# Attention gates and outputs stored by channel, reciprocals spread on GpSimd, and a filter network on 128 partitions

## The chip, the core and the metric

The kernel runs on one core of one Trainium2 chip. A core has TensorE (PE, with its weight load PEld), VectorE (DVE), ScalarE (ACT), GpSimd (POOL) and SyncE (SP). Each engine has a queue of its own that runs in order; engines wait for each other by semaphores. PE writes to PSUM only, and POOL reads and writes SBUF only. The metric is the device time of one execution in microseconds (us), the median of several runs.

## The reference, cut to what matters

One inference step of two layers on 1024 sample tokens and 128 prompt tokens, width 1024. Layer one is a Hyena long convolution, whose filters come from a small network; layer two is latent attention with 16 heads and a SiLU gate on each branch.

```python
def hyena_filters(L, w1, b1, freq, w2, b2, w3):      # L = 1024 and 128
    z = ...                                           # (L, 33) positions
    hdn = jnp.sin(fr * (z @ w1 + b1))                 # 33 -> 64
    hdn = jnp.sin(fr * (hdn @ w2 + b2))               # 64 -> 64
    h = hdn @ w3                                      # 64 -> 2048
    ...

def mla_latent(h, ckv_ctx, kpe_ctx, ...):
    q_a, kv_a, k_pe, gate = split(h @ w_in)           # 384, 256, 32, 1024
    q = rmsnorm(q_a) @ w_qb                           # 16 heads x (64 + 32)
    q_pe, k_pe = axial rope of the 32
    k_nope, v = expand(rmsnorm(kv_a)), with 256 cached tokens appended
    o = softmax(q k / sqrt(96)) @ v                   # 16 heads x 64
    return (o * silu(gate)) @ w_o
```

The prompt is attended to by itself alone, without rope. Residual, output gate and a last rmsnorm follow.

## The kernel before, in words

Nine tiles of 128 tokens (T = 1152; tile 8 is the prompt). Large products run as three matmuls on split operands: `hi` copies a value to the rounded type fp32r, `lo` subtracts that copy from the value, and hi x hi, hi x lo and lo x hi add up in one PSUM bank. So each operand costs an evacuation by two engines.

Start (`hyena`, L644 on): nine tiles of x are loaded, normalized and turned; eight 1 MB pieces of `ada_w` give scale and shift; `modulate` (L206) makes the parts hT and lT. Two input weights are applied early (L715): the first accumulates in three banks `ip_ps`, the second in three banks `sf_ps`, which the turned x and then the filter network use before it. `filters` (L235) runs the network with `sin_layer` (L211), feature on partition: 33 and 64 rows, tokens in pieces of 512, 512 and 128. A piece is a matmul, seven DVE instructions (L219 to L224, three of them L102) that scale and reduce the angle, and ACT's sine. Its result `hs` holds the high part in rows 0 to 63 and the low part in rows 64 to 127.

Attention (`mla`, L844): `w_out` ends the Hyena layer and normalizes its tiles one after the other into lhh and lhl (the hT and lT of this layer). `mla_gate` (L949) multiplies them with a quarter of the gate weights, for each token tile: tokens on PSUM's partitions, 256 channels in its columns. It stores silu of it to DRAM tiles `gate0` to `gate8`, one per token tile. The first quarter is emitted after `w_out`, the others after `mla_in`. `attend` (L959) copies the turned rope keys `kr` to four places of kT, six of the copies by DMA on SP. `attention` (L1049) runs four groups of four heads, each in four chunks of 256 queries (the last with 128 prompt queries as well), each chunk in four units of one head, order 0, 2, 1, 3. On PE, DVE and ACT the order inside is written out by hand (`ORDER`, `tc.manual_schedule`); POOL's and SP's queues, and all the rest, are ordered at build time by a planner that simulates the program. A unit does the scores and softmax of the next head, and transposes, products with V and the close of its own. Step `r` takes the reciprocal of the sums (L1177); `et` (L1182) adds V's high and low halves into `ot`, 64 channels by 256 queries, and POOL multiplies the gate by the reciprocals, one number per query, so queries stand on partitions there. After a second, odd unit, `fm` (L1211) turns the pair's `ot` to queries on partitions, `fx` (L1214) copies it from PSUM and POOL multiplies it with the gate. After four units `store_o` writes 256 queries by 256 channels to `og` tiles, one per token tile. The next chunk's `q_proj` (L1028) makes its rope from two copies, in which halves of 32 rows are swapped by DMA on SP, and POOL multiplies and splits; the first chunk's part stands ahead of all scores.

Output (`out_load`, `out_t`, `mla_out`): POOL splits the first half of `w_o` during the last chunk. `out_t` loads `og`, turns it by PE transposes (`split_t`, L835) to channels on partitions and splits it with ACT and DVE: first for tiles 0 to 3, then 8, 4, 5, then 6, 7. Then `mm3` (L616) projects.

Of the kernel before, what the change touches and what calls it, by code (L numbers as in the profile page):

```python
# [17 lines left out]
P = 128  # L18
# [57 lines left out]
class K:  # L76
# [134 lines left out]
    def sin_layer(self, pool, ps, w, src, kk, out, col):  # L211

        for o, n in ((0, 512), (512, 512), (1024, 128)):
            pt = ps.tile([P, 512], F32, name=STAG[0], tag=STAG[0], bufs=STAG[1])[0:64]
            self.PE.matmul(pt[:, :n], w, src[:kk, o:o + n], start=True, stop=True)
            x = pool.tile([64, 512], F32, name="mlp_x", tag="mlp_x")
            q = pool.tile([64, 512], F32, name="mlp_q", tag="mlp_q", bufs=1)
            x, q = x[:, :n], q[:, :n]
            self.V.tensor_scalar(x, pt[:, :n], self.fcol[:, col:col + 1], self.fcol[:, 0:1], ALU.add, ALU.mult)  # L219
# [15 lines left out]
    def filters(self, pool, ps, hs):  # L235

        nc, tc, a = self.nc, self.tc, self.a
        zt = pool.tile([33, T], F32, name="zt", tag="ft", bufs=2)
        nc.scalar.dma_start(zt, a["zemb"])
        w1 = pool.tile([33, 64], F32, name="w1", bufs=1)  # L240
        nc.scalar.dma_start(w1, a["f_w1"])
        w2 = pool.tile([64, 64], F32, name="w2", bufs=1)
        nc.scalar.dma_start(w2, a["f_w2"])
        fcol = pool.tile([64, 3], F32, name="fcol", bufs=1)
        nc.scalar.dma_start(fcol, a["f_cols"])
        self.fcol = fcol
# [597 lines left out]
    def mla(self, lh, hT, lT, wp, wo, gd, AB):  # L844
        tc, dr = self.tc, self.dr
        GD = [dr.tile([P, D], F32, name=f"gate{t}") for t in range(NT)]
        OG = [dr.tile([P, D], F32, name=f"og{t}") for t in range(NT)]
        with self.pool("mcs", space=PSUM) as ps:
# [99 lines left out]

    def mla_gate(self, h, pool, ps, hT, lT, GD, bufs):  # L949
        wh, wl = self.load_w(self.a["wm_g"][h], pool, 256, "wm", bufs, raw_bufs=2, step=1, tag_raw="wm_raw",  # L950
                             size=336 if h else 256)
        for t in range(NT):
            pt = ps.tile([P, 512], F32, name="wo_ps", tag="wo_ps", bufs=4)
            self.mm3(pt[:, :256], hT, lT, slice(P * t, P * t + P), wh, wl, 8)
            g = pool.tile([P, 256], F32, name="gsil", bufs=GB)
            self.S.activation(g, pt[:, :256], AF.Silu)
            (self.nc.sync if h else self.nc.scalar).dma_start(GD[t][:, 256 * h:256 * h + 256], g)
# [70 lines left out]
    def q_proj(self, m, c, part):  # L1028
# [8 lines left out]
        for i in range(2):  # L1037
            x = m["pool"].tile([P, 384], F32, name=f"rot{i}", bufs=1)[:, :n]
            self.S.copy(x, pt[:, :n])
            for r in range(0, P, 64):  # L1040
                y = r + 32 * i, r + 32 - 32 * i
                self.nc.sync.dma_start(x[y[1]:y[1] + 32], x[y[0]:y[0] + 32])
            self.tt(x, x, c["rq"][:, :n], ALU.mult, self.G)
            for r, j in ((slice(0, 64), i), (slice(64, P), i + 2)):
                self.hi("pool", qh[r, j, :n], x[r])
                self.lo("pool", ql[r, j, :n], x[r], qh[r, j, :n])
        yield

    def attention(self, m):  # L1049
# [3 lines left out]
        def start(n):  # L1053
# [6 lines left out]
            for i in range(2):  # L1060
                nc.sync.dma_start(gt[:, i], m["GD"][q0 // P + i][:, 256 * G:256 * G + 256])
# [3 lines left out]
            return c, [self.q_proj(m, c, p) for p in range(3)]  # L1065
# [90 lines left out]
    def step(self, m, u, what, n):  # L1156
# [19 lines left out]
        elif what == "r":  # L1176
            self.V.reciprocal(u["sm"][:, :, 3], u["sm"][:, :, 0])  # L1177
# [4 lines left out]
        elif what == "et":  # L1182
            self.halves(m["ot"], u["po"][:, :256], m["ov"], u["odd"])
            for i in range(2):
                o = gt[:, i, VH * j:VH * j + VH]
                self.G.tensor_scalar(o, o, u["sm"][:, i, 3:4], None, ALU.mult)  # L1186
            if u["odd"]:
                g = gt.rearrange("p i (e j d) -> p i e j d", e=2, d=VH)[:, :, :, j % 2]
                m["fin"] = [u["po"][:, 256:512], m["ot"], g, u if u["last"] else None]
        elif what in ("fm", "fx"):  # L1190
            self.finish(m, what)
# [12 lines left out]
    def finish(self, m, what):  # L1204
# [3 lines left out]
        pt, ot, g, u = m["fin"]  # L1208
# [11 lines left out]
    def store_o(self, m, c):  # L1220
        for i in range(2):
            self.nc.sync.dma_start(m["OG"][c["q0"] // P + i][:, 256 * c["G"]:256 * c["G"] + 256], c["gt"][:, i])

    def prompt(self, m, c):
# [4 lines left out]
        o = slice(256 * c["G"], 256 * c["G"] + 256)  # L1229
        g = pool.tile([P, 256], F32, name="gp", bufs=1)  # L1230
        self.nc.sync.dma_start(g, m["GD"][8][:, o])
# [20 lines left out]
        self.lo("dve", l, pt, h)  # L1252
        self.V.reciprocal(sm, sm)
        self.tt(heads(g), heads(g), sm.unsqueeze(2).broadcast_to([P, 4, VH]), ALU.mult, self.G)
# [9 lines left out]
        for odd in range(2):  # L1264
            self.half(ov, heads(po)[:, odd::2], odd)
        yield
        for odd in range(2):
            self.halves(ot, heads(po)[:, odd::2], ov, odd)
        yield
        for i in range(2):  # L1270
            self.PE.transpose(po[:, P * i:P * i + P], ot[:, i], self.ident)
        yield
        yield
        self.tt(g, po[:, :256], g, ALU.mult)
        self.nc.sync.dma_start(m["OG"][8][:, o], g)
# [32 lines left out]
    def out_t(self, ps, OG, pool, tiles, oh, ol):  # L1308
        for b in range(0, 8, 2):
            src = []  # L1310
            for t in tiles:
                x = pool.tile([P, 256], F32, name="og_in", bufs=4)
                self.nc.sync.dma_start(x, OG[t][:, P * b:P * b + 256])
                src.append(x)
            for k in range(2):
                self.split_t(ps, [x[:, P * k:P * k + P] for x in src], 0, oh, ol, b + k)

    def out_head(self, ps, OG, e):
        self.out_t(ps, OG, e["pool"], range(4), *e["o"])

    def mla_out(self, ps, OG, e, gd):
        nc, a = self.nc, self.a
        with self.pool("ew", 2, side="left") as pool:
# [5 lines left out]
            for tiles in (range(4), (8, 4, 5), (6, 7)):  # L1329
                if tiles[0]:  # L1330
                    oh, ol = (pool.tile([P, 8, 384], F32R, name=n) for n in ("oh", "ol"))
                    self.out_t(ps, OG, pool, tiles, oh, ol)
# [118 lines left out]
def _layout(i):  # L1451
# [16 lines left out]
    out["wm_a"], out["wm_g"] = _ktiles(wi[:, :672], 336), _ktiles(wi[:, 672:], 256)  # L1468
# [8 lines left out]
    out["w_o"] = _ktiles(i["mla_w_o"][0], 512)  # L1477
# [19 lines left out]
```

## Time and profile before

| | us |
|---|---|
| median of 3 runs (lowest, highest) | 1804.11 (1803.85, 1807.5) |
| profiled execution | 1801.83 |
| its span | 1799.7 |
| PE busy | 1747.2 (97%) |
| DVE busy | 1249.6 (69%) |
| ACT busy | 1088.1 (60%) |
| POOL busy | 528.1 (29%) |

The span runs from the first instruction to the last; the profiled execution's own time adds what lies around it. A row of the trace gives the start and the length in us, the engine, the line of the kernel, the operation, the tile written and the tiles read, and the shapes. Behind it stands, in brackets, how long the engine sat idle before and what released it. An engine name with a q is its queue issuing a DMA.

### The profile page before, as it was taken

The page shows a single profiled execution, that of the slowest core. Times are in us where ns is not written, and L with a number is a line of the kernel's source. Part 1 is how long each engine was busy: PE and PEld are TensorE (multiplying, and loading weights), DVE is VectorE, ACT ScalarE, POOL GpSimd, SP SyncE. Part 2 cuts the span into 40 slices and gives each one's busy share as a digit, 9 for nine tenths or more (in the row PEclk, how much of TensorE's full clock was granted, in tenths as well). Part 3 has the DMA queues.
Part 4 walks back from the last instruction along what each step waited for, and adds up shares of the span by engine and source line. Part 5 has one row for each costly group of instructions (what it writes and reads, how often), then busy time and mean ns, then how long its engine had stood idle before and what let it go on. Part 6 is the DMA issues. An engine that isn't in the chain of part 4 may idle for free.

```text
span 1799.7 us, 30649 instructions
## 1 busy us (share of the span) xinstructions
PE 1747.2 (97%) x11064; PEld 1568.3 (87%) x11064; DVE 1249.6 (69%) x2526; ACT 1088.1 (60%) x2582; POOL 528.1 (29%) x748
## 2 busy tenths in 40 slices
PE   6999999999999999999999899999999999999998
PEld 4888988999899888889999799999989999998786
DVE  3948797898886797432241587878787787878454
ACT  7655565755664234234452588878887887888332
POOL 2433333343344120331000233333423242344100
PEclk9999999999999999999999999999999999999999
DMA  8333332111122857322122300110101010002541
GB/s 325 94 113 106 115 107 74 51 54 45 61 101 92 293 188 260 135 82 91 55 67 80 90 27 24 35 29 20 35 25 29 20 37 17 28 27 68 187 135 71
DMA packets 94704, 157.15 MB, mean 87 GB/s; under 512 B 11671, under 2 KB 64183, under 8 KB 92760
## 3 DMA queue, kind: packets, MB, share of 16 engines
q1 hardware_dynamic: 91744, 151.78, 25.5%
q10 hardware_dynamic: 2552, 3.39, 0.6%
q8 instruction: 87, 1.43, 0.3%
q14 instruction: 65, 0.53, 0.1%
q0 software_dynamic: 256, 0.02, 0.0%
HBM read 113.89 MB, written 36.73 MB: 84 GB/s over the span
## 4 chain that ended last, share of the span: by engine, by line
PE 75%; DVE 11%; DMA 4%; ACT 4%; issue 3%; POOL 2%; SPq 0%; ACTq 0%; DVEq 0%; POOLq 0%
PE wo_ps L616 18%; PE wo_ps L1289 12%; PE ip_ps L415 11%; PE av_ps L1174 8%; PE nm_ps L1162 7%; PE wo_ps L989 5%; PE iv_ps L545 3%; PE df_ps L364 2%; DMA wi_raw<-w_in 2%; PE nm_ps L1021 1%; DVE pr_o L99 1%; DVE cv L102 1%; PE ada_ps L113 1%; POOL wi_l L96 1%; DVE mx L1292 1%
## 5 line engine op out<-in xcount | busy, mean ns | idle before, releaser
L1289 PE MATMUL wo_ps<-kT,qT 128*128 128x512 f32 (+1 forms) x1152 | 279.7, 373 | 8.1 <-ACT prob L1296 4.1
L1296 ACT ACTIVATE prob<-wo_ps,mx 128x512 f32<-128x512 f32 (+1 forms) x384 | 234.0, 618 | 17.9 <-DVE mx L1294 16.0
L88 ACT ACTIVATE pt_h<-nm_ps 128x512 fp32r<-128x512 f32 x324 | 192.9, 599 | 70.5 <-PE nm_ps L1162 63.2
L1292 DVE TENSOR_REDUCE mx<-wo_ps 128x1 f32<-128x512 f32 (+1 forms) x384 | 212.8, 594 | 27.9 <-PE wo_ps L1289 27.1
L1289 PEld LDWEIGHTS wo_ps<-kT,qT 128*128 128x128 f32 x1152 | 188.2, 190 | 42.6 <-ACT prob L1296 14.0
L96 DVE TENSOR_TENSOR pt_l<-nm_ps,pt_h 128x512 fp32r<-128x512 f32 x324 | 210.5, 682 | 13.2 <-ACT pt_h L88 13.1
L1162 PE MATMUL nm_ps<-ident,prob 128*128 128x128 f32 x1280 | 191.5, 272 | 0.0
L96 POOL TENSOR_TENSOR wi_l<-wi_raw,wi_h 128x512 fp32r<-128x512 f32 x64 | 110.7, 1730 | 253.0 <-ACT wi_h L88 237.0
L1162 PEld LDWEIGHTS nm_ps<-ident,prob 128*128 128x128 f32 x1280 | 150.1, 140 | 8.4
L415 PE MATMUL ip_ps<-lT,wi_h 128*128 128x384 f32 x720 | 152.3, 341 | 0.0
L415 PE MATMUL ip_ps<-hT,wi_h 128*128 128x384 f32 x720 | 150.8, 344 | 0.6 <-ACT cv L497 0.6
L415 PE MATMUL ip_ps<-hT,wi_l 128*128 128x384 f32 x720 | 150.7, 341 | 0.0
L1174 PE MATMUL av_ps<-pt_h,Vt 128*128 128x256 f32 x640 | 138.0, 297 | 0.0
L1174 PE MATMUL av_ps<-pt_l,Vt 128*128 128x256 f32 x640 | 135.4, 293 | 0.3 <-DVE pt_l L96 0.2
L415 PEld LDWEIGHTS ip_ps<-hT,wi_h 128*128 128x128 f32 x720 | 126.3, 190 | 6.9 <-issue 3.0
L415 PEld LDWEIGHTS ip_ps<-hT,wi_l 128*128 128x128 f32 x720 | 126.0, 188 | 7.1 <-issue 3.8
L415 PEld LDWEIGHTS ip_ps<-lT,wi_h 128*128 128x128 f32 x720 | 127.9, 190 | 3.7 <-issue 0.8
L616 PE MATMUL wo_ps<-wm_h,lhh 128*128 128x256 f32 (+1 forms) x432 | 125.9, 296 | 1.7 <-ACT wm_h L88 1.4
L616 PE MATMUL wo_ps<-wm_h,lhl 128*128 128x256 f32 (+1 forms) x432 | 127.1, 295 | 0.0
L616 PE MATMUL wo_ps<-wm_l,lhh 128*128 128x256 f32 (+1 forms) x432 | 126.7, 294 | 0.0
L1186 POOL TENSOR_SCALAR gt<-gt,sm 128x64 f32<-128x64 f32 x128 | 54.9, 443 | 225.3 <-DVE sm L1177 224.0
L99 POOL TENSOR_TENSOR pr<-ev 128x256 f32<-128x256 f32 x72 | 83.6, 1166 | 126.0 <-ACT ev L372 77.5
(338 smaller groups left out, 4060.1 us busy)
## 6 DMA issues: line engine op xcount, KB each, us to landing
wi_raw<-w_in SPq DMA_DIRECT2D x64, 256.0 KB, 2.6
ada_w<-ada_w SPq DMA_DIRECT2D x12, 1024.0 KB, 10.0
ada_w<-ada_w SPq DMA_DIRECT2D x24, 512.0 KB, 4.0
x_in<-xs SPq DMA_DIRECT2D x16, 512.0 KB, 5.3
PS<-pr_o SPq DMA_DIRECT2D x64, 128.0 KB, 1.9
pi_raw<-PS SPq DMA_DIRECT2D x32, 256.0 KB, 4.8
YD<-yv SPq DMA_DIRECT2D x8, 576.0 KB, 3.3
y<-YD SPq DMA_DIRECT2D x8, 576.0 KB, 8.7
```

Source lines behind the costliest of these rows:

```text
L88: self.S.activation(out, src, AF.Copy)
L96: e.tensor_tensor(out, src, hi.bitcast(F32), ALU.subtract)
L99: (eng or self.V).tensor_tensor(out, x, y, op)
L415: mm = self.PE.matmul(pt, w[:, k, :], x[c][:, k, :], start=s == 0 and k == 0, stop=s == 2 and k == 7)
L616: self.PE.matmul(pt, x[k][:, sl], w[:, k, :], start=s == 0 and k == 0, stop=s == 2 and k == kt - 1)
L989: self.PE.matmul(pt[:, :n], x[:, k, o:o + P], y[:, k, c], start=s == 0 and k == 0, stop=s == 2 and k == kt - 1)
L1162: self.PE.transpose(pt[:, P * i:P * i + P], u["p"][i % 2][n // 2][:, P * (2 * (n % 2) + i // 2):P * (2 * (n % 2) + i // 2) + P], self.ident)
L1174: self.PE.matmul(u["po"][:, :256], m["V"][:, 2 * n + e, j, :], u[n][1 + s][:, 256 * e:256 * e + 256], start=n == first and e + s == 0, sto ...
L1186: self.G.tensor_scalar(o, o, u["sm"][:, i, 3:4], None, ALU.mult)
L1289: self.PE.matmul(pt[:, :n], x[:, j, P * i:P * i + P], y[:, j, o:o + n], start=s == 0, stop=s == 2)
L1292: self.V.tensor_reduce(mx[:, b:b + 1], c["s", i, b][:, :n], AX.X, ALU.max)
L1296: self.S.activation(c["p"][i][b], c["s", i, b][:, :n], AF.Exp, bias=c["mx"][i][:, 3:4], accum_out=c["sm"][:, i, b:b + 1])
```

## The change

- The network takes two halves of 576 tokens at once, on rows 0 to 63 and 64 to 127: w1 as two blocks in zeroed tiles, w2 block diagonal, in two pieces of 288 columns a layer. POOL fills zt, w1 and w2 with zeros first, and the low half of `hs` is put together by five instructions where two were.
- The gate product is turned: weights stand still and tokens stream, 384 at a time, so that gate and output tiles in DRAM are one per 128 channels. Channels of w_in's gate and of w_o are reordered on the host to fit.
- The reciprocals are spread by POOL over 64 columns per head (`rr`), and PE transposes `rr` where it transposed `ot`. POOL multiplies the gate by it, then by `ot`, and issues the store, once per pair.
- `out_t` loads channels on partitions: no transposes. POOL splits the first four tiles, ACT and DVE the rest.
- The first chunk's rope swaps halves with DVE copies from PSUM; DVE multiplies, ACT and DVE split. kT's six DMAs go by POOL's queue.

```diff
-        for o, n in ((0, 512), (512, 512), (1024, 128)):
+        n = T // 4
+        for o in (0, n):
+            pt = ps.tile([P, 512], F32, name=STAG[0], tag=STAG[0], bufs=STAG[1])[:, :n]
+            for i, w in enumerate(ws):
+                self.PE.matmul(pt, w, src[:, 2 * n * i + o:2 * n * i + o + n], start=i == 0, stop=i == len(ws) - 1)
...
+        zt = pool.tile([P, T], F32, name="zt", bufs=1)
+        self.G.memset(zt, 0.0)
+        nc.scalar.dma_start(zt[0:33], a["zemb"])
...
+        for i in range(2):
+            r = slice(64 * i, 64 * i + 64)
+            nc.scalar.dma_start(w1[0:33, i, r], a["f_w1"])
+            nc.scalar.dma_start(w2[r, r], a["f_w2"])
+            nc.scalar.dma_start(fcol[r], a["f_cols"])
...
+        self.hi("act", hs[top, 0:n], h2[top])
+        self.hi("act", hs[low, n:T], h2[low])
+        self.S.copy(hs[top, n:T], hs[low, n:T].bitcast(F32))
+        self.lo("dve", hs[low, 0:n], h2[top], hs[top, 0:n])
+        self.lo("dve", hs[low, n:T], h2[low], hs[low, n:T])
...
-        for t in range(NT):
-            self.mm3(pt[:, :256], hT, lT, slice(P * t, P * t + P), wh, wl, 8)
+        for o in range(0, T, 384):
+            for i in range(2):
+                w = slice(P * i, P * i + P)
+                pt = ps.tile([P, 512], F32, name="wo_ps", tag="wo_ps", bufs=4)[:, :384]
+                for k in range(8):
+                    for s, (a, b) in enumerate(((wh, hT), (wl, hT), (wh, lT))):
+                        self.PE.matmul(pt, a[:, k, w], b[k][:, o:o + 384], start=s == 0 and k == 0, stop=s == 2 and k == 7)
...
-                    nc.sync.dma_start(x.bitcast(F32), y)
+                    nc.gpsimd.dma_start(x.bitcast(F32), y)
...
+                if first:
+                    self.V.tensor_copy(x[y[1]:y[1] + 32], pt[y[0]:y[0] + 32, :n])
+                else:
+                    self.nc.sync.dma_start(x[y[1]:y[1] + 32], x[y[0]:y[0] + 32])
+            self.tt(x, x, c["rq"][:, :n], ALU.mult, None if first else self.G)
...
+            if not u["odd"]:
+                m["rr"] = pool.tile([P, 2, P], F32, name="rr", bufs=2)
+            r = u["sm"][:, :, 3:4]
+            self.V.reciprocal(r, u["sm"][:, :, 0:1])
+            self.G.tensor_copy(m["rr"][:, :, VH * u["odd"]:VH * u["odd"] + VH], r.broadcast_to([P, 2, VH]))
...
-            for i in range(2):
-                o = gt[:, i, VH * j:VH * j + VH]
-                self.G.tensor_scalar(o, o, u["sm"][:, i, 3:4], None, ALU.mult)
...
-                self.PE.transpose(pt[:, P * i:P * i + P], ot[:, P * i:P * i + P], self.ident)
+                self.PE.transpose(pt[:, P * i:P * i + P], rr[:, i], self.ident)
         else:
             ov = m["ov"]
             self.S.copy(ov, pt)
-            self.tt(g, ov.rearrange("p (i e d) -> p i e d", e=2, d=VH), g, ALU.mult, self.G)
-            if u:
-                self.store_o(m, u)
+            self.tt(g, ov, g, ALU.mult, self.G)
+            self.tt(g, ot, g, ALU.mult, self.G)
+            self.nc.gpsimd.dma_start(out, g)
...
+        for k in range(8):
+            x = pool.tile([P, 512 if n == 512 else 384], F32, name="og_in", tag="og_in", bufs=2 if n == 512 else 3)[:, :n]
+            d = 0
+            for o, w in parts:
+                self.nc.sync.dma_start(x[:, d:d + w], OG[k][:, o:o + w])
+                d += w
+            self.hi(hi, oh[:, k, :n], x)
+            self.lo(lo, ol[:, k, :n], x, oh[:, k, :n])
```

## Rows read from the trace of the kernel before

**Rows 1.** The page's busy time per engine: us, share of the span, instructions
```profile
PE 1747.2 (97%) x11064; PEld 1568.3 (87%) x11064; DVE 1249.6 (69%) x2526; ACT 1088.1 (60%) x2582; POOL 528.1 (29%) x748
```

**Rows 2.** Stretches: length, busy PE, PEld, DVE, ACT, POOL, clock, DMA
```profile
34.70:59.30 24.60, 24.22 (x153) 13.68 (x152) 22.49 (x48) 17.43 (x36) 13.56 (x18) 1.00 0.39 143
59.30:75.90 16.60, 16.60 (x97) 16.58 (x97) 15.95 (x31) 10.93 (x21) 6.37 (x7) 1.00 0.25 70
...
996.00:1027.00 31.00, 25.07 (x153) 22.57 (x152) 15.55 (x33) 19.25 (x45) 7.58 (x14) 0.94 0.47 109
1027.00:1624.00 597.00, 594.53 (x4183) 541.26 (x4182) 481.46 (x1017) 485.01 (x1259) 213.10 (x438) 1.00 0.09 27
1624.00:1677.00 53.00, 52.12 (x379) 47.50 (x379) 42.62 (x92) 43.59 (x117) 25.29 (x45) 1.00 0.19 58
1677.00:1785.30 108.30, 104.81 (x481) 84.25 (x479) 47.23 (x90) 28.67 (x70) 1.33 (x3) 0.98 0.44 153
```

**Rows 3.** The network's tile: ns min/median/max, first and last start, forms
```profile
L102 DVE SCALAR_TENSOR_TENSOR mlp_x<-mlp_q,mlp_x x18: 276/674/1380, 41.1 to 74.6; 64x512 f32<-64x512 f32 x12, 64x128 f32<-64x128 f32 x6
L219 DVE TENSOR_SCALAR mlp_x<-sf_ps,fcol x6: 396/794/802, 39.0 to 69.3; 64x512 f32<-64x512 f32 x4, 64x128 f32<-64x128 f32 x2
```

**Rows 4.** Line 715, the two early weights, and what PE waited for
```profile
L715 PE MATMUL sf_ps<-hT,wi_l x24: 336/336/336, 59.8 to 75.7; 128*128 128x384 f32 x24
...
  DVE lT L96: 3.0, 6
```

**Rows 5.** Timeline of the start, a POOL write
```profile
37.31 0.51 POOL L90 TENSOR_SCALAR hT<-nm_h 128x384 fp32r<-128x384 f32 x1 [1.03 <-ACT nm_h L206]
```

**Rows 6.** Line 616 in a stretch of gates: length, PE, PEld, clock, DMA
```profile
949.80:992.10 42.30, 42.30 (x359) 42.27 (x358) 1.00 0.23 70
```

**Rows 7.** Timeline, first gate group and tile 8's last piece
```profile
813.07 0.28 PE L616 MATMUL wo_ps<-wm_h,lhh 128*128 128x256 f32 x1
...
836.84 0.29 DVE L96 TENSOR_TENSOR lhl<-nm_h,lhh 128x128 fp32r<-128x128 f32 x1 [0.28 <-POOL lhh L90]
```

**Rows 8.** The chain of waits, transposes: start, us, what
```profile
797.48 0.66 PE nm_ps L181 x6
```

**Rows 9.** Timeline where attention starts
```profile
999.46 1.78 SPq L972 DMA_DIRECT2D kT<-krl  x1
...
1005.27 0.64 ACT L1039 COPY rot<-wo_ps 128x256 f32<-128x256 f32 x2
...
1012.45 0.72 POOL L99 TENSOR_TENSOR rot<-rot,rope_q 128x256 f32<-128x256 f32 x1 [79.14 <-DMA rot<-rot]
...
1013.71 1.66 PE L1289 MATMUL wo_ps<-kT,qT 128*128 128x512 f32 x7 [3.48 <-POOL qT L90]
```

**Rows 10.** POOL's DMA issues, by tile: ns min/median/max
```profile
L146 POOL DMA_DIRECT2D gate_rows<-ada_row x8: 518/552/756, 96.9 to 667.9; - x8
```

**Rows 11.** The gate tile of attention: ns min/median/max
```profile
L1186 POOL TENSOR_SCALAR gt<-gt,sm x128: 438/443/449, 1039.0 to 1677.2; 128x64 f32<-128x64 f32 x128
...
L99 POOL TENSOR_TENSOR gt<-ov,gt x32: 725/734/744, 1049.2 to 1684.3; 128x256 f32<-128x256 f32 x32
```

**Rows 12.** Timeline, the closest pair of transposes to its reciprocal
```profile
1662.40 0.16 DVE L1177 RECIPROCAL sm<-sm 128x2 f32<-128x2 f32 x1
1662.72 0.62 POOL L90 TENSOR_SCALAR wo_h<-w_raw 128x512 fp32r<-128x512 f32 x1 [1.77 <-DMA w_raw<-w_o]
...
1663.42 1.29 POOL L96 TENSOR_TENSOR wo_l<-w_raw,wo_h 128x512 fp32r<-128x512 f32 x1
...
1665.14 0.38 PE L1211 MATMUL av_ps<-ident,ot 128*128 128x128 f32 x2
```

**Rows 13.** Timeline, a POOL split beside DVE's cv
```profile
77.63 1.41 DVE L102 SCALAR_TENSOR_TENSOR cv<-u,cols,cv 128x1153 f32<-128x1153 f32 x1
...
78.02 2.18 POOL L96 TENSOR_TENSOR wi_l<-wi_raw,wi_h 128x512 fp32r<-128x512 f32 x1 [3.88 <-ACT wi_h L88]
```

**Rows 14.** Timeline, the last split of w_o's second half
```profile
1717.77 0.69 DVE L96 TENSOR_TENSOR wo_l<-w_raw,wo_h 128x512 fp32r<-128x512 f32 x1 [0.52 <-ACT wo_h L88]
```

More of the change, by code (lines that the diff above doesn't have):

```diff
@@ L208, in modulate, with sin_layer @@
         self.lo("dve", lT, h, hT)
-    def sin_layer(self, pool, ps, w, src, kk, out, col):
-        for o, n in ((0, 512), (512, 512), (1024, 128)):
[L214 to L219, printed above, removed]
+    def sin_layer(self, pool, ps, ws, src, out, col):
+        n = T // 4
[3 more added lines that the diff above has]
+                self.PE.matmul(pt, w, src[:, 2 * n * i + o:2 * n * i + o + n], start=i == 0, stop=i == len(ws) - 1)
+            x = pool.tile([P, n], F32, name="mlp_x", tag="mlp_x")
+            q = pool.tile([P, n], F32, name="mlp_q", tag="mlp_q")
+            self.V.tensor_scalar(x, pt, self.fcol[:, col:col + 1], self.fcol[:, 0:1], ALU.add, ALU.mult)
             self.V.tensor_scalar(q, x, 1.0 / TWO_PI, MAGIC, ALU.mult, ALU.add)
@@ L845, in mla @@
         tc, dr = self.tc, self.dr
-        GD = [dr.tile([P, D], F32, name=f"gate{t}") for t in range(NT)]
-        OG = [dr.tile([P, D], F32, name=f"og{t}") for t in range(NT)]
+        GD = [dr.tile([P, T], F32, name=f"gate{k}") for k in range(8)]
+        OG = [dr.tile([P, T], F32, name=f"og{k}") for k in range(8)]
         with self.pool("mcs", space=PSUM) as ps:
@@ L1026, in v_proj, with q_proj @@
         self.lo("dve", V[:, t, :, VH:P], pv, V[:, t, :, 0:VH])
-    def q_proj(self, m, c, part):
+    def q_proj(self, m, c, part, first=False):
         n, qh, ql = c["n"], c["qh"], c["ql"]
@@ L1064, in start @@
             c = dict(G=G, q0=q0, n=n, qh=qh, ql=ql, gt=gt, rq=rq)
-            return c, [self.q_proj(m, c, p) for p in range(3)]
+            return c, [self.q_proj(m, c, p, G + q0 == 0) for p in range(3)]
         def unit(c, x):
@@ L1228, in prompt @@
         qh, ql = (x[:, :, 256:384] for x in (c["qh"], c["ql"]))
-        o = slice(256 * c["G"], 256 * c["G"] + 256)
-        g = pool.tile([P, 256], F32, name="gp", bufs=1)
-        self.nc.sync.dma_start(g, m["GD"][8][:, o])
+        g = pool.tile([P, 2, P], F32, name="gp", bufs=1)
+        for i in range(2):
+            self.nc.sync.dma_start(g[:, i], m["GD"][2 * c["G"] + i][:, T - P:T])
         pt = ps.tile([P, 512], F32, name="wo_ps", tag="wo_ps", bufs=4)
@@ L1252, in prompt @@
         self.lo("dve", l, pt, h)
+        rr = pool.tile([P, 2, P], F32, name="rrp", bufs=1)
         self.V.reciprocal(sm, sm)
-        self.tt(heads(g), heads(g), sm.unsqueeze(2).broadcast_to([P, 4, VH]), ALU.mult, self.G)
+        for i in range(2):
+            self.G.tensor_copy(rr[:, i].rearrange("p (e d) -> p e d", d=VH), sm[:, i::2].unsqueeze(2).broadcast_to([P, 2, VH]))
         yield
@@ L1264, in prompt @@
         for odd in range(2):
-            self.half(ov, heads(po)[:, odd::2], odd)
+            self.half(ov, heads(po)[:, 2 * odd:2 * odd + 2], odd)
         yield
         for odd in range(2):
-            self.halves(ot, heads(po)[:, odd::2], ov, odd)
+            self.halves(ot, heads(po)[:, 2 * odd:2 * odd + 2], ov, odd)
         yield
         for i in range(2):
-            self.PE.transpose(po[:, P * i:P * i + P], ot[:, i], self.ident)
+            self.PE.transpose(po[:, P * i:P * i + P], rr[:, i], self.ident)
         yield
         yield
-        self.tt(g, po[:, :256], g, ALU.mult)
-        self.nc.sync.dma_start(m["OG"][8][:, o], g)
+        self.tt(g, po[:, :256].rearrange("p (i c) -> p i c", c=P), g, ALU.mult)
+        self.tt(g, ot, g, ALU.mult, self.G)
+        for i in range(2):
+            self.nc.sync.dma_start(m["OG"][2 * c["G"] + i][:, T - P:T], g[:, i])
     def score(self, m, c, what, i, b):
@@ L1306, in out_load, with out_t @@
         return e
[L1308 to L1319, printed above, removed]
+    def out_t(self, OG, pool, parts, oh, ol, hi, lo):
+        n = sum(w for _, w in parts)
+        for k in range(8):
[6 more added lines that the diff above has]
+            self.lo(lo, ol[:, k, :n], x, oh[:, k, :n])
     def mla_out(self, ps, OG, e, gd):
@@ L1328, in mla_out @@
             nc.sync.dma_start(fin, a["fin_norm"].partition_broadcast(P))
-            for tiles in (range(4), (8, 4, 5), (6, 7)):
-                if tiles[0]:
+            for tiles, parts in ((range(4), None), ((8, 4, 5), ((1024, P), (512, 256))), ((6, 7), ((768, 256),))):
+                if parts:
                     oh, ol = (pool.tile([P, 8, 384], F32R, name=n) for n in ("oh", "ol"))
-                    self.out_t(ps, OG, pool, tiles, oh, ol)
+                    self.out_t(OG, pool, parts, oh, ol, "act", "dve")
                 else:
@@ L1476, in _layout @@
     out["w_kvb"] = _ktiles(np.concatenate(parts, 2).reshape(KVL, 2048), 512)
[L1477 removed]
+    out["w_o"] = _ktiles(np.ascontiguousarray(i["mla_w_o"][0].reshape(4, 4, VH, D)[:, by_pair]).reshape(D, D), 512)
     out["kv_norm"], out["fin_norm"] = i["mla_kv_norm"][0], i["final_norm"]
```

54 lines of the change are left out of this document (22 added, 32 removed).

## The prediction

> **What bounds the kernel now.** First the page's busy shares: PE 97%, DVE 69%, ACT 60%, POOL 29% [rows 1]. TensorE is busy almost without a break, so an edit is worth what it takes off PE, or what it takes out of PE's few gaps. Then the table of stretches, to find the gaps [rows 2]. The attention, 1027 to 1624, has 594.5 us of PE in 597.0: nothing is to be gained there, and something can be lost. Gaps lie at 996 to 1027 (5.9 us of 31.0, where attention starts) and 1677 to 1785.3 (3.5 us, the output projection); 34.7 to 59.3 reads 24.2 of 24.6 us, but a PE stretch with many short waits looks fuller than it is, because the ends of matmuls are modelled. Third the stretches themselves: the tiles and lines of the filter network, the timelines where gates, attention and output begin, and the chain of waits.
>
> **The network of the start.** Six pieces (512, 512 and 128 columns, two layers, 64 partitions) of seven DVE instructions become four of 288 columns on 128 partitions. L102 takes 276 ns at 128 columns and 674 ns at 512, so about 1.04 ns a column and 0.44 us at 288; L219 goes from 396 to 794 ns, 0.56 us at 288 [rows 3]. The three single-input instructions are bounded by L102. Before: 4 x (0.79 + 6 x 0.67) + 2 x (0.40 + 6 x 0.28) = 23.4 us at most; after 4 x (0.56 + 6 x 0.44) = 12.8. So DVE loses some 10 us between 38 and 76, where it is busy 22.5 of 24.6 and 16.0 of 16.6 us [rows 2]. What of it reaches PE? The second early weight accumulates in the same three PSUM buffers as the network, and its 72 matmuls fill PE from 59.3 to 75.9 without a gap (the third of their three kinds starts at 59.8 and last at 75.7); before them PE sat 3.0 us waiting for DVE's lT [rows 4]. An earlier network lets those matmuls fill the short waits before 59.3. I take -2.5 us. The ends: 0 if the arrival of the ada weights sets the pace, -6 if most waits of that stretch close, and +1.5 the other way: zt's zero fill stands on POOL ahead of zt's DMA, which ACT issues together with three more DMAs. The fill is at most 1.5 us, three times POOL's 0.51 us for 384 columns [rows 5], and lies beside the first loads of x; that cover is gone only if ACT still waits for it when its first squares could run.
>
> **The gates.** The columns streamed stay the same (864 x 256 = 576 x 384); the overhead of each matmul is saved. 359 matmuls of 256 columns took 42.3 us, 118 ns each [rows 6]; 97 matmuls, nearly all of 384 columns, took 16.6 us, 171 ns each [rows 2]. For all four gates: 864 x 118 = 101.9, 576 x 171 = 98.5, so -3.4 us. Against it: the first gate is what PE does while tile 8 is still being normalized. It starts at 813.07, and tile 8's last piece is written at 837.1 [rows 7]. Before, eight of nine groups don't need tile 8; now four of six. Four groups take 4 x 24 x 0.171 = 16.4 us, with 24 transposes at 0.11 (0.66 us for 6 [rows 8]) 2.6 more, so PE is there at 832.1 and needs the last piece 3.6 us later, at 835.7: up to 1.4 us too early. I take -2 (ends -3.5 and +2). Silu and stores become fewer and wider and stay hidden behind PE.
>
> **The first queries.** Before: ACT copies at 1005.27, then the swap DMAs, POOL starts the product at 1012.45, and the first scores start at 1013.71 after 3.48 us of idle PE [rows 9]. After, from the same 1005.27: ACT copy 0.32, two DVE copies and a DVE product at 256 columns, 0.41 each by L102's slope, ACT's high part 0.4: ready at about 1007.5, before the last v_proj matmuls are through. The 3.5 us of wait go, and part of the other 2.4 us of gaps in 996 to 1027. What is late next is the first softmax, which DVE must reduce: the edit adds ten DVE instructions of about 0.4 us (four copies, two products, four low parts), 4 us, in a stretch where DVE is busy 15.6 of 31.0 us, and they stand among the low parts of V. I take -4; ends 0 (DVE gives it all back) and -6 (the whole gap). The six kT copies move from SP to POOL. On SP one held the queue for 1.78 us [rows 9], with gt, rope_q and the swaps behind it; SP is now free for those loads. POOL has nothing else to do then, since the first rope leaves it too. Its issues in the trace are small ones, 0.52 to 0.76 us [rows 10]; six cost 3 to 5 us by these, 11 by the 1.78. The second unit needs them, some 10 us later.
>
> **Attention.** PE, DVE and ACT keep their counts: two transposes per pair of heads, now of the spread reciprocals. POOL, per pair: before 4 x 0.443 + 0.734 = 2.5 us [rows 11]; after, two copies of 128 columns (0.44 to 0.73 each by the same rows), two products and one DMA issue (0.52 to 1.78), together 2.9 to 4.7 us. At 213 of 597 us busy POOL has room. But the transposes now wait for POOL's copy. In the closest pair they come 2.58 us after the reciprocal's end, with two weight splits of 0.62 and 1.29 us just ahead: the copy would end at about 1665.2, and the transposes start at 1665.14 [rows 12]. I take +1 for the last pairs (ends 0 and +8).
>
> What rows show to be slowed is POOL beside two-input DVE work from SBUF: a split of 128x512 takes 1.29 us alone [rows 12], 2.18 us beside DVE's cv [rows 13]. In attention POOL's product stays within 725 to 744 ns 32 times with DVE 80% busy [rows 2, 11], so DVE's readers of PSUM don't hold it. The Trainium skill, SBUF — State Buffer (SBUF: two separate sides, in its part on the bandwidth-pool intuition), says that a DMA issued from POOL can be starved of descriptors while DVE holds the shared port, 620 ns becoming about 3100. By that rule the 32 new stores would hold POOL some 32 x 2.5 = 80 us longer, an estimate; the rows show no such DVE work in attention, and I go by them.
>
> **The output.** 72 transposes go (eight blocks of nine tiles) at 0.11 us [rows 8]: 7.9 us, 64 of them after 1677. The 3.5 us of idle PE there are waits for og_in and its turned copies; they go if the parts are ready. For the first four tiles that is now POOL's work: 8 x (0.62 + 1.29) = 15.3 us [rows 12], in a stretch (1624 to 1677) where POOL is busy 25.3 of 53.0 us, so 40.6 of 53. It fits, with queueing behind w_o's loads. Next late is the second half of w_o: its last split ends at 1718.5 [rows 14]. The projection without transposes and gaps is 108.3 - 7.0 - 3.5 = 97.8 us for 432 matmuls, 0.226 each; four tiles of the first half take 96 x 0.226 = 21.7 us, so PE asks for the second half from 1698.7 to 1704. Its loads stood behind og_in on SP and now move up too. I let these two cost 3.4 of the 11.4 us: -8 (ends -11 and +4).
>
> **Sum.** -2.5 - 2 - 4 + 1 - 8 = -15.5. The profiled execution took 1801.83 us (span 1799.7), 2.3 below the median 1804.11 of the runs; so 1786.3 for a profile like it and 1789 for the median.
>
> **Rivals.**
> *Only the instructions go.* The start is paced by arriving weights, DVE gives the first rope back in its softmax, and the tail keeps its waits under new names. Left: 7.9 + 2 = 10 us, 1794. For it: PE already reads 24.2 of 24.6 us at the start. Against: the 3.48 us of the rope have one plain cause. 0.20.
> *POOL ends last in the output.* POOL takes the splits of the first four tiles only after the attention. Then 15.3 us of POOL stand in PE's path against 11.4 saved: the tail is 3.9 longer instead of 8 shorter, 1801. For it: POOL's order is fixed ahead of time, and w_o's splits already wait for their loads (1.77 us at 1662.72). Against: the og_in tiles can be loaded long before 1677. 0.14.
> *PE waits for POOL's reciprocals* (slower). One mechanism: each of the 32 pairs of transposes finds the copy not yet done, because POOL's queue is busy with the rope of the next queries, weight splits, the second product or the store's issue. At 1 us each it costs 32 us: 1821. It outweighs the gain from 0.6 us each (19 us). For it: POOL is in order, and its queue is not ordered by hand, as PE's is. Against: the gap is 2.58 us at its closest, and a copy needs at most 0.73. 0.12. The page named above would make the store's issue the likeliest cause of it.
> That an edit doesn't do what it says (the kT copies or zt's fill delay what stands behind them) lies in the first rival.
>
> **How the numbers follow.** Forecast 0.54 (its own range 1782 to 1795), rivals 0.20, 0.14, 0.12. A measurement can tell 0.2%, 3.6 us: faster is below 1800.5. The forecast, the first rival and 0.06 of the second lie there, 0.80; 0.08 of the second is the same; the third is slower, 0.12. The range 1780 to 1801 leaves out the third and the edges of the others.
>
> **What would show it.** The stretch from the end of attention to the last projection falls to about 100 us, with under 3 us of idle PE; the first scores follow the ACT copy by under 4 us; gate matmuls read 0.17 us at 384 columns; the second early weight starts before 59.3; PE has no idle time in front of the pair transposes (L1211 before). The prediction is wrong if POOL shows up as the releaser of PE in attention or output, or if stretches that the edits don't touch change by more than 3 us.

## The result and the profile after

| | before | after |
|---|---|---|
| median us (lowest, highest), 4 runs each | 1805.8 (1803.85, 1807.52) | 1784.68 (1783.28, 1786.28) |
| ratio, 95% interval | | 0.9881 (0.9863, 0.9899) |
| profiled execution, its span | 1801.83, 1799.7 | 1784.39, 1782.2 |

The change takes 21.5 us (18.2 to 24.7) off; the forecast was 15.5, to 1789 us. Faster was right; the sum was 6 us short, and its parts fell otherwise than forecast. The page's busy row after, for [rows 1]:

```profile
PE 1728.2 (97%) x10704; PEld 1555.8 (87%) x10704; DVE 1245.5 (70%) x2515; ACT 1087.0 (61%) x2566; POOL 550.1 (31%) x771
```

PE lost 19.0 us of busy time, about what the span lost (17.5), and POOL gained 22.0. Where that lies is read by landmarks: the first and last start of the matmuls of one line cut the span into stages. Worked out so from both traces, in us:

| stage | before | after | gain | forecast |
|---|---|---|---|---|
| start to last matmul of the early weights | 75.7 | 71.2 | 4.5 | 2.5 |
| to the first matmul of w_out (convolutions) | 631.2 | 635.6 | -4.4 | 0 |
| to the first gate matmul | 106.2 | 106.1 | 0.1 | 0 |
| to the last gate matmul (with the latent projection) | 182.7 | 182.8 | -0.1 | 2 |
| to the first scores | 17.9 | 15.3 | 2.6 | 4 |
| to the last scores | 655.0 | 654.3 | 0.7 | -1 |
| to the last projection matmul | 122.4 | 108.6 | 13.8 | 8 |
| to the end | 8.6 | 8.3 | 0.3 | 0 |

The stretches after, for [rows 2] (length, busy PE, PEld, DVE, ACT, POOL, clock, DMA share, GB/s):

```profile
33.50:51.90 18.40, 16.76 (x132) 11.95 (x132) 16.80 (x39) 14.28 (x30) 9.30 (x14) 1.00 0.50 193
51.90:71.50 19.60, 19.60 (x114) 19.23 (x112) 12.25 (x25) 12.26 (x23) 7.00 (x13) 1.00 0.29 91
71.50:116.00 44.50, 38.65 (x235) 33.57 (x235) 23.90 (x32) 25.14 (x51) 17.42 (x11) 1.00 0.39 124
...
996.00:1024.00 28.00, 25.02 (x159) 21.92 (x157) 19.59 (x43) 21.58 (x49) 3.87 (x8) 1.00 0.48 111
...
1620.00:1667.00 47.00, 46.37 (x333) 42.19 (x333) 38.69 (x84) 39.05 (x106) 37.92 (x57) 1.00 0.33 98
1667.00:1774.00 107.00, 105.77 (x482) 86.05 (x480) 53.12 (x101) 32.19 (x81) 5.18 (x9) 1.00 0.41 143
```

The third row is new: right behind the early weights PE is idle for 5.9 of 44.5 us. Before, it was full there:

```profile
75.90:120.00 44.10, 44.10 (x274) 39.10 (x274) 25.02 (x31) 25.22 (x48) 16.68 (x13) 1.00 0.42 138
```

What PE waits for between 71.5 and 707 us after (us in total, times, longest):

```profile
PE ip_ps L426 <- ACT wi_h L88: 5.9, 3, 2.3
PE df_ps L375 <- DVE ab_lo L96: 5.2, 7, 1.7
```

The first of these two waits, for the split of the third input weight, doesn't exist before; 3.8 of its 5.9 us lie in that third row. In the last two rows of the stretches PE is nearly full (46.4 of 47 and 105.8 of 107 us) and the clock 1.00; POOL is busy 37.9 of 47 us just ahead of the projection.

### The profile page after: what moved, and what is told of

The parts are those of the page before. It is cut to its first block, busy times and chain, and to the rows that moved or that the text cites. A ratio compares the mean times of both kernels' runs of the same rounds, so it can differ in the third digit from the quotient of the medians.

```text
span 1782.2 us, 29982 instructions
## 1 busy us (share of the span) xinstructions
PE 1728.2 (97%) x10704; PEld 1555.8 (87%) x10704; DVE 1245.5 (70%) x2515; ACT 1087.0 (61%) x2566; POOL 550.1 (31%) x771
## 4 chain that ended last, share of the span: by engine, by line
PE 75%; DVE 13%; DMA 4%; ACT 3%; issue 3%; POOL 2%; SPq 0%; DVEq 0%; ACTq 0%; POOLq 0%
PE wo_ps L627 14%; PE wo_ps L1309 12%; PE ip_ps L426 10%; PE av_ps L1193 9%; PE nm_ps L1181 7%; PE wo_ps L970 5%; PE wo_ps L1005 5%; PE iv_ps L556 3%; PE df_ps L375 2%; DMA wi_raw<-w_in 2%; DVE pr_o L99 2%; DVE cv L102 1%; PE nm_ps L1037 1%; DVE O L102 1%; POOL wi_l L96 1%
## 5 line engine op out<-in xcount | busy, mean ns | idle before, releaser
L96 POOL TENSOR_TENSOR wi_l<-wi_raw,wi_h 128x512 fp32r<-128x512 f32 x64 | 121.6, 1900 | 243.7 <-ACT wi_h L88 238.2
L99 POOL TENSOR_TENSOR pr<-ev 128x256 f32<-128x256 f32 x72 | 77.0, 1075 | 130.0 <-ACT ev L383 75.4
L1193 PEld LDWEIGHTS av_ps<-pt_l,Vt 128*128 128x128 f32 x640 | 97.6, 188 | 8.2 <-DVE pt_l L96 2.1
L1193 PEld LDWEIGHTS av_ps<-pt_h,Vt 128*128 128x128 f32 x640 | 97.9, 189 | 0.2
L102 DVE SCALAR_TENSOR_TENSOR cv<-u,cols,cv 128x1153 f32<-128x1153 f32 x48 | 75.7, 1578 | 11.8 <-ACT cv L451 11.7
L1200 POOL COPY rr<-sm 128x128 f32<-128x128 f32 x64 | 18.4, 288 | 202.4 <-DVE sm L1199 201.8
```

The source lines that it names most:

```text
L96: e.tensor_tensor(out, src, hi.bitcast(F32), ALU.subtract)
L99: (eng or self.V).tensor_tensor(out, x, y, op)
L102: self.V.scalar_tensor_tensor(out, x, s, y, op0, op1)
L1193: self.PE.matmul(u["po"][:, :256], m["V"][:, 2 * n + e, j, :], u[n][1 + s][:, 256 * e:256 * e + 256], start=n == first and e + s == 0, sto ...
```

## The experiments

Each changes the kernel after, or before where it says so. Ratios are against the kernel before on the same chip, with 95% intervals; the kernel after has 0.9881.

**The network.** Two runs: after with `sin_layer` and `filters` of before, and before with those of after (below).

```
-        for o, n in ((0, 512), (512, 512), (1024, 128)):
+        n = T // 4
+        for o in (0, n):
...
+        self.sin_layer(pool, ps, (w1[:, 0], w1[:, 1]), zt, h1, 1)
+        self.sin_layer(pool, ps, (w2,), h1, h2, 2)
...
```

> The changed kernel with the filter network of before (64 partitions, six pieces); all else as changed. Theory A: the network brought the end of the early weights forward by 4.4 us, but the waits for the third in-projection weight gave it back before 707 us, so the network is worth 0 (-2 to +2): about 1784.7. Theory B, the prediction's term: it is worth 2.5 us, up to the 4.4 seen at the early weights: 1787 to 1789.

> The kernel before with the network on 128 partitions as its only change. Theory A (gained at 76 us, given back by 707): early weights end near 71.5, the w_out projection starts within 1 us of 706.9, time as before, about 1805 (1803 to 1807). Theory B (the gain stays): 1801 to 1803.

Taken back: 0.9892 (0.9876, 0.9908), against after not to be told apart. Alone: 0.9985 (0.9976, 0.9995), 2.7 us faster (0.9 to 4.3). Theory A, nothing left, falls by the second: the prediction's 2.5 us is inside. The first pair of profiles by itself would have said A, with 706.9 and 706.8 us at the first w_out matmul. But over the profiles of this study that landmark is 706.9, 707.0, 707.3 and 710.0 with the old network, and 704.1 to 709.0 (nine profiles, mean 705.9) with the new one: it scatters by 5 us with the same source ahead of it, so the 1.9 us between the means show nothing by themselves. The wait of 5.9 us for wi_h is there in the run with the network alone too. So the network gains 4.5 us at the early weights and 2.7 us in the time. The idle PE of the third row above, and this wait in it, is the first place where some of the gain can go; that it is all of it isn't shown.

**The third weight's wait.** Its staging buffer holds half a weight, and the next half is loaded when that is split.

```
-            for k in (slice(0, 4), slice(4, 8)):
-                raw = pool.tile([P, 4, P], F32, name="wi_raw", bufs=1)
+            for k in (slice(0, 2), slice(2, 4), slice(4, 6), slice(6, 8)):
+                raw = pool.tile([P, 2, P], F32, name="wi_raw", bufs=2)
```

> The changed kernel with each in-projection weight loaded in four pieces of 128 KB through two staging buffers, in place of two pieces of 256 KB through one (the same SBUF). Theory A: after the earlier network TensorE waits 3.8 us for the third weight (72 to 78 us) and 2.1 us for a later one, because a piece can only be loaded when the one before is split; with two buffers most of the 5.9 us goes and stays gone: 1780 to 1782. Theory B: the stage of the convolutions gives back what is gained at its start, as in the two profiles compared so far (706.9 and 706.8 us at its end), and pays for twice as many loads: 1784.7 within 2.

0.9899 (0.9879, 0.9919): no gain, and against after not to be told apart. Its waits of PE, same columns:

```profile
PE df_ps L375 <- ACT ab_lo L371: 6.3, 2, 6.0
PE ip_ps L426 <- ACT wi_h L88: 4.8, 2, 3.5
```

Of 5.9 us 4.8 stay, so the single staging buffer was not the cause of most of it, and a wait of 6.0 us for a transform's split is new. Theory A falls. Why the stage's end scatters is open.

**The first queries.** Three runs: the rope as before (`first` never set), the kT copies back on SP, and before with the kT copies on GpSimd alone.

```
-            return c, [self.q_proj(m, c, p, G + q0 == 0) for p in range(3)]
+            return c, [self.q_proj(m, c, p) for p in range(3)]
```

```
-                    nc.gpsimd.dma_start(x.bitcast(F32), y)
+                    nc.sync.dma_start(x.bitcast(F32), y)
```

The third is the second edit the other way, in the kernel before.

> The changed kernel with the first queries' rope as before (swap DMAs on SP, product and split on POOL); the kT copies stay on POOL. Theory A: the first scores come some 2.8 to 3.5 us later and nothing behind takes it up: 1787.5 to 1788.5. Theory B (DVE gives the first rope back in the first softmax, so that undoing it costs nothing): 1784.7.

> The changed kernel with the six kT copies issued from SP again. Theory A: with the first swaps gone from SP nothing urgent stands behind them, no change within 1 us: 1784 to 1786. Theory B: on SP they hold rope_q and gt, the first rope and the first scores come 1 to 3 us later: 1786 to 1788.

> The kernel before with the six kT copies issued from GpSimd as its only change (the first queries' rope stays on SP, GpSimd). Theory A: on SP these six held rope_q and the four swaps, and that was the first scores' delay; from the last gate matmul to the first scores 15 to 16 us in place of 17.9, and 4 us in all with what the second unit gains: 1801.5. Theory B: the gain needs the rope on the vector engine: 17 to 18 us, and 1805 as before.

Rope as before: 0.9873 (0.9856, 0.9891), so with kT on GpSimd the rope edit gains nothing that can be measured. kT back on SP: 0.99 (0.9884, 0.9916), some 3 us slower by the ratios, but the intervals overlap. kT alone: 0.999 (0.998, 0.9999), 1.8 us faster (0.2 to 3.6). From the last gate matmul to the first scores the five take: before 17.9, before with kT moved 16.4, after with kT on SP 16.1, after without the rope 15.3, after 15.3. With neither edit in the changed kernel (the run below, channels alone) it is 17.6. So the two edits overlap: the rope alone takes 1.5 us off, kT alone 2.3, both 2.3. The timelines say why. After with kT on SP (start, us, engine, line, what; idle before and its releaser):

```profile
997.22 1.80 SPq L988 DMA_DIRECT2D kT<-krl  x1
...
1005.28 0.43 SPq L1082 DMA_DIRECT2D rope_q<-rope_q  x1
...
1008.60 0.43 DVE L99 TENSOR_TENSOR rot<-rot,rope_q 128x256 f32<-128x256 f32 x1 [2.51 <-DMA rope_q<-rope_q]
...
1009.53 1.92 PE L1309 MATMUL wo_ps<-kT,qT 128*128 128x512 f32 x8 [2.48 <-ACT qT L88]
```

The vector engine has the halves swapped, and waits for the rope's table, which SP issues behind six kT copies and two gate loads. With kT on GpSimd and the old rope:

```profile
1001.63 2.33 SPq L1082 DMA_DIRECT2D rope_q<-rope_q  x1
...
1005.82 2.50 SPq L1061 DMA_DIRECT2D rot<-rot  x4
...
1009.26 0.73 POOL L99 TENSOR_TENSOR rot<-rot,rope_q 128x256 f32<-128x256 f32 x1 [12.12 <-DMA rot<-rot]
...
1010.53 2.69 PE L1309 MATMUL wo_ps<-kT,qT 128*128 128x512 f32 x12 [0.80 <-POOL qT L90]
```

Counted from the last gate matmul, the table is issued 6.4 us behind it in place of 11.9. The swaps go 0.4 us behind ACT's copies (1005.42), and PE's wait is 0.8 in place of 3.48 us [rows 9]. In the kernel before, the swaps went 2.6 us behind ACT's copies [rows 9]:

```profile
1007.92 3.09 SPq L1042 DMA_DIRECT2D rot<-rot  x4
```

So most of the delay was what stood ahead in SP's queue, not the swap by DMA; the new rope gains only where that queue is still held. Theory A of the last run is right in kind and too high: in the kernel before, PE still waits 2.0 us, and the stage to the last scores gains nothing (656.6 us).

What differs behind the first scores goes with TensorE's clock. The 30 us from the first scores on, columns as in the stretches: after, before, before with kT moved, after with kT on SP:

```profile
1011.00:1041.00 30.00, 26.63 (x166) 22.55 (x166) 23.18 (x50) 22.88 (x58) 10.74 (x19) 1.00 0.10 30
1013.70:1043.70 30.00, 26.88 (x159) 23.23 (x160) 20.46 (x42) 19.80 (x51) 16.12 (x28) 0.94 0.10 32
1012.30:1042.30 30.00, 26.97 (x147) 22.95 (x147) 19.02 (x39) 18.42 (x48) 16.15 (x28) 0.89 0.12 35
1009.50:1039.50 30.00, 26.96 (x155) 23.36 (x156) 21.62 (x47) 21.03 (x51) 10.77 (x19) 0.89 0.11 30
```

A granted clock of 1.00 is 2.4 GHz throughout; below it PE ran a part of the stretch at 1.2 GHz, after waits for the queries (none flagged, 3.5, 2.0 and 2.5 us) and for the first softmax (2.4 to 2.7 us). The stage to the last scores takes 654.3, 655.0, 656.6 and 657.6 us in this order. So in these profiles the 3.3 us that kT on SP loses behind the first scores come with the lower clock; whether every execution has it isn't shown.

**Channels alone.** After with the three edits above undone together: network, first rope and kT as before.

> Only gates and outputs by channel with the reciprocals spread by GpSimd; network, first queries' rope and kT copies as before. Theory A (by the two traces: tail -13.7, gates 0, attention 0): before less 13 to 14.5, about 1791.5. Theory B (the prediction's terms -2 for the gates, +1 for the attention, -8 for the output): before less 9, about 1796.

0.9913 (0.9894, 0.9933): 15.7 us (12.1 to 19.1), theory A. Its output stage takes 108.5 us. The three parts measured by themselves, 15.7 + 2.7 + 1.8, make 20.2 of the 21.5 us; the intervals of the parts are wider than the rest.

**Who splits the first four output tiles.**

```
-                    self.out_t(OG, e["pool"], ((0, 512),), *e["o"], "pool", "pool")
+                    self.out_t(OG, e["pool"], ((0, 512),), *e["o"], "act", "dve")
```

> The changed kernel with the splits of the first four output tiles on ACT and DVE in place of POOL. Theory A: what POOL does beside the last attention (8 x 1.9 us) is free only there; ACT and DVE are each some 83% busy from 1620 to 1667, their 8 x 0.6 and 8 x 0.7 us delay the last softmax or come after it: 3 to 10 us slower, 1788 to 1795. Theory B: it is the missing transposes alone that gain, and any engine hides the splits: 1784.7 within 1.5.

0.9929 (0.9913, 0.9944), 8.7 us slower than after by the ratios: theory A. The output stage is the same 108.6 us; the stage to the last scores grows from 654.3 to 661.7. A stretch of it, columns as above:

```profile
1621.90:1660.00 38.10, 32.18 (x223) 27.95 (x221) 31.41 (x62) 30.07 (x81) 19.90 (x32) 1.00 0.36 112
```

PE is idle for 5.9 of 38.1 us, where after has 0.6 in 47. Between 1600 and 1690 us it waits 2.2 us for pt_l, a split by DVE, 2.0 for ACT's exponentials and 1.2 for a copy by ACT, none of which it waits for after: the attention's work and the output's splits share these two engines.

**How near GpSimd's reciprocals are to the path.** The second copy of a pair is made 8 times, in a second run 15 times; the values stay the same.

```
-            self.G.tensor_copy(m["rr"][:, :, VH * u["odd"]:VH * u["odd"] + VH], r.broadcast_to([P, 2, VH]))
+            for _ in range(8 if u["odd"] else 1):
+                self.G.tensor_copy(m["rr"][:, :, VH * u["odd"]:VH * u["odd"] + VH], r.broadcast_to([P, 2, VH]))
```

> The changed kernel with the second copy of each pair of reciprocals made eight times, which holds GpSimd for 7 x 0.29 = 2.0 us more ahead of each of the 32 pairs of transposes. The traces' slack between copy and transposes is 1.08 and 1.99 us in two pairs and 2.66 or more in thirty. Theory A (the wait is free up to its slack): only the one pair pays, 1 us: 1785 to 1787. Theory B (GpSimd's queue is already what paces these pairs): 10 us or more slower.

> As the run with eight copies, but fifteen: 14 x 0.29 = 4.1 us more. By the slacks of the trace 25 of 32 pairs are then late, by 27.6 us in sum. Theory A (TensorE is in order and nothing takes the wait up): 1784.7 + 28 = 1812, 1806 to 1818. Theory B (later work takes the waits up, so the rival of the prediction was never a danger): under 1790.

1.0233 (1.0213, 1.0253), 62 us above after by the medians, and 1.1214 (1.1196, 1.1233), 239 us. Theory A was wrong in both by far; B of the first is right in sign only, B of the second wrong. PE's waits for the copies, first with eight, then with fifteen:

```profile
PE av_ps L1231 <- POOL rr L1201: 45.8, 21, 9.2
```

```profile
PE av_ps L1231 <- POOL rr L1201: 186.4, 28, 25.0
```

One pair of the run with eight, on POOL's timeline:

```profile
1216.17 0.64 POOL L1201 COPY rr<-sm 128x128 f32<-128x128 f32 x2 [3.85 <-DVE sm L1199]
1217.68 0.20 POOL L99 TENSOR_TENSOR sm<-sm 128x2 f32<-128x2 f32 x1 [0.86 <-ACT prob L1317]
1217.81 0.29 POOL L1201 COPY rr<-sm 128x128 f32<-128x128 f32 x1
1218.06 0.20 POOL L99 TENSOR_TENSOR sm<-sm 128x2 f32<-128x2 f32 x1
1218.19 1.71 POOL L1201 COPY rr<-sm 128x128 f32<-128x128 f32 x5
```

Between the copies stand the next unit's sums, and the first waits 0.86 us for ACT's exponentials. So the eight copies, 2.3 us by themselves, take 3.7 us, and the longest waits, 8.0 and 9.2 us, lie where the splits of w_o and of the output tiles stand between too. The rest of the 62 us is not in these waits (45.8 us); the mean granted clock of the execution also fell, from 0.997 to 0.988, and to 0.949 with fifteen copies. A slack read from a trace holds for that order of instructions only; POOL's order is planned, and here other instructions came to stand between the copies.

**The latent projection's weights, and gate 0.** Two runs, one edit each:

```
-            wh, wl = self.load_w(a["wm_a"][h], wpool, 336, "wm", 2, raw_bufs=2, step=1, tag_raw="wm_raw")
+            with self.urgent():
+                wh, wl = self.load_w(a["wm_a"][h], wpool, 336, "wm", 2, raw_bufs=2, step=1, tag_raw="wm_raw")
```

```
-        for o in range(0, T, 384):
+        for o, n in ((0, 384), (384, 384), (768, 384)) if h else ((0, 512), (512, 384), (896, 256)):
...
```

> The changed kernel with the loads and splits of the latent projection's weights (mla_in) given the higher priority that other stages use. Theory A: their first split stands on ACT behind the last two silus of gate 0, and TensorE waits 1.6 and 0.8 us for it; ahead of them these 2 us go: 1782.7. Theory B: the weights' loads, 3.3 us for two slices, pace that stage, and the wait only moves to the next slice: 1784.7 within 1.5.

> The changed kernel with gate 0 in column blocks of 512, 384 and 256 in place of three of 384 (the same 144 matmuls, and the same columns streamed). Theory A: the block that needs tile 8 comes last and is 256 wide, so TensorE reaches it 2.6 us later, and its wait for tile 8 (0.6 us flagged, 1.3 in the length of the stage) goes: 1783.4. Theory B: the stage ends at the weights of the latent projection anyway: 1784.7 within 1.

0.9887 (0.9869, 0.9905) and 0.9884 (0.9866, 0.9901): both come out at the time of theory B. But in the first the split still stands behind the two silus, so it tests neither theory. From the first gate matmul to the first of the latent projection it takes 30.5 us after, 30.5 and 30.9 in these two, 29.1 before. With the second edit PE's flagged wait for tile 8 falls from 0.6 to 0.3 us, and the stretch is no shorter. No version of the study beats the changed kernel by what can be measured.

## Why the prediction was right, and where its terms were not

**Network, -2.5.** Right in size by the run that has it alone. The tile's rows answer to [rows 3] (ns min/median/max, first and last start):

```profile
L102 DVE SCALAR_TENSOR_TENSOR mlp_x<-mlp_q,mlp_x x12: 443/457/1511, 39.9 to 57.8; 128x288 f32<-128x288 f32 x12
L220 DVE TENSOR_SCALAR mlp_x<-sf_ps,fcol x4: 566/567/573, 38.5 to 53.9; 128x288 f32<-128x288 f32 x4
```

0.44 and 0.56 us at 288 columns were forecast. The second weight's matmuls start at 52.0 us, not 59.3, and end at 71.2. What was missing is the next one in line. The first weight's last matmul moved only from 70.5 to 69.7 us, and the third weight's first split did not move at all, before and then after:

```profile
72.08 0.62 ACT L88 ACTIVATE wi_h<-wi_raw 128x512 fp32r<-128x512 f32 x1
```

```profile
69.48 1.28 ACT L276 ACT_TABLE_LOAD   x1
70.78 1.26 ACT L276 ACTIVATE dec<-trow,cols 128x1152 f32<-128x1152 f32 x1
...
72.30 0.63 ACT L88 ACTIVATE wi_h<-wi_raw 128x512 fp32r<-128x512 f32 x1
```

After, a table load and `dec`, a part of the filters, stand on ACT ahead of it, 2.5 us together. No run tests whether another order of ACT would give the rest.

**Gates, -2.** Nothing came. In 25.0 us of gates alone (960 to 985) stand 145 matmuls of 384 columns: 0.172 us each, near the 0.171 taken from [rows 2], so some -2.6 for all four gates. Behind the latent projection the stage does shrink, from 86.2 to 82.8 us, but ahead of it the gain is given back: gate 0 and the wait behind it take 30.5 us in place of 29.1, the latent projection 69.5 in place of 67.5. Its weights' first split stands on ACT behind gate 0's last two silus and their stores, which now both fall at the very end:

```profile
841.49 0.87 ACT L972 ACTIVATE gsil<-wo_ps 128x384 f32<-128x384 f32 x2 [4.40 <-DMA c_ckv<-c_ckv]
842.01 0.81 ACTq L973 DMA_DIRECT2D gate<-gsil  x2
842.87 0.86 ACT L88 ACTIVATE wm_h<-wm_raw 128x336 fp32r<-128x336 f32 x2 [0.51 <-ACT gsil L972]
...
843.40 0.88 PE L627 MATMUL wo_ps<-wm_h,lhh 128*128 128x336 f32 x4 [1.60 <-ACT wm_h L88]
```

Of the latent projection's 2.0 us, 1.3 are in two more waits for these splits (2.9 us in three waits, 1.4 in one before). The step that failed: the prediction looked at tile 8 and not at this split. The run with priority did not move it, so what holds it there is open.

**First queries, -4.** The place was right (2.6 us to the first scores), the cause was wrong, and that the size came near was luck. The step that failed is that the swap DMAs make the delay, and that kT's move costs 3 to 5 us at nothing gained but room for loads. [Rows 9] had it: a kT issue of 1.78 us on SP, with the table and the swaps behind. On GpSimd each takes 0.51 to 0.62 us. The Trainium skill, DMA: Bandwidth & Descriptors (Issuing engine by pattern), puts simple loads and stores on SP's queue; its Rules for kernel authors add that spreading DMAs over issuers saves only issue time. Here the issue time was the point, 1.78 us against 0.5.

**Attention, +1.** No wait of PE for POOL, and nothing that can be told from 0: this pair is 0.7 us better, but five more profiles with the attention of after take 654.8 to 655.0 us, as before (655.0), all with 0.94 in the 30 us from the first scores, where after's own profile has 1.00. The closest pair, for [rows 12]:

```profile
1639.95 0.16 DVE L1199 RECIPROCAL sm<-sm 128x2 f32<-128x2 f32 x1
1640.53 1.28 POOL L96 TENSOR_TENSOR o<-og_in,o 128x512 fp32r<-128x512 f32 x1
1641.76 0.29 POOL L1200 COPY rr<-sm 128x128 f32<-128x128 f32 x1
...
1643.13 0.38 PE L1230 MATMUL av_ps<-ident,rr 128*128 128x128 f32 x2
```

The copy is 0.29 us, below the 0.44 to 0.73 taken. The third rival's mechanism is real all the same: with 2 us more on POOL per pair 21 of the 32 pairs of transposes wait, 2.2 us each on average and up to 9.2, where the rival had 1 us.

**Output, -8.** 13.8 came. The step that failed is the allowance of 3.4 us for late splits: only one wait of 1.2 us, for w_o's second half, is left. All of the 11.4 us of transposes and waits is gone but for that 1.2, and 1.5 us are from the clock, which I had not counted. Before, PE's waits of 1.47 us for og_in and 0.67 us for its copy, with four transposes between, are followed by seven matmuls at the lower of the two clock levels, 1.2 GHz (kernel before, four of them, then the stretch with its mean granted clock):

```profile
1701.78 0.77 PE L616 MATMUL wo_ps<-wo_h,o 128*128 128x512 f32 x1 [0.67 <-ACT o L88]
1702.34 0.63 PE L616 MATMUL wo_ps<-wo_l,o 128*128 128x512 f32 x1
...
1704.47 0.57 PE L616 MATMUL wo_ps<-wo_h,o 128*128 128x512 f32 x1
1704.88 0.40 PE L616 MATMUL wo_ps<-wo_l,o 128*128 128x512 f32 x1
```

```profile
1701.50:1710.00 8.50, 8.22 (x33) 6.77 (x34) 3.69 (x6) 2.31 (x6) 0.00 (x0) 0.80 0.85 312
```

They start 0.43 us apart, 3.1 us for seven; at 0.233 us, the pace at 2.4 GHz, it would be 1.6. After, the whole stretch reads 1.00. For the last 2 us the trace names no wait; they went together with the transposes, and no run separates them. My stretch also ended too early: 25 matmuls lie behind 1785.3, and one takes 0.233 us, not 0.226. The second rival (POOL's splits only after the attention) did not happen: they end by 1652.6, and PE begins the projection at 1667.0, between the last pairs.

**The signs it named.** Four held: gate matmuls read 0.172 us, the second early weight starts at 52.0 us, PE never waits for the pair transposes, and POOL releases PE nowhere in attention or output. Three did not. The stretch of the projection is 107.0 us, with 1.2 us of idle PE, not about 100: the 25 matmuls were missing, and the projection begins while the attention's last matmuls still run. The first scores follow ACT's first copy (1005.88) by 5.1 us, not by under 4. And the convolutions, which no edit touches, changed by 4.4 us, over the 3 us allowed; they take in the early weights' gain and scatter by 5 us, so by itself this doesn't speak against the mechanism.

## What to carry to other kernels

Before an edit is credited with a wait, look at what else stands in the queue that the wait ends on: here moving six DMAs to another queue did at least what a rewritten rope was meant to do. Work on an idle engine is free only in the order in which it is planned; a slack read between two instructions is no allowance for a third. Compare kernels stage by stage by landmarks, over several profiles: stages that repeat closely (w_out 106.1 to 106.2 us in all profiles, the new output 108.4 to 109.0 in ten) show effects that the total hides, and one that scatters by 5 us says nothing from one pair. Where a dense stage differs between two profiles, look at the granted clock first: a stretch at the lower level can pass for an effect of the edit.

## What the runs showed of the hardware

The DMAs that GpSimd issues in the attention stay short (ns min/median/max):

```profile
L1236 POOL DMA_DIRECT2D og<-gt x32: 604/612/624, 1047.6 to 1694.0; - x32
```

The Trainium skill, SBUF — State Buffer (SBUF: two separate sides), warns that such a DMA can be starved while DVE holds the shared port. The 80 us that the prediction estimated by it did not come: with DVE busy 223.0 of 276 us (1024 to 1300) none of the 32 issues took over 0.63 us. DVE reads mostly PSUM there, so no run here shows the rule's own case.
